# The product of stick weight and running product on GpSimd in the attention stage

## The chip, the cores and the metric

The kernel runs on one core of a Trainium2 chip. The core's engines are TensorE (PE in the profile, its weight loads PEld), VectorE (DVE), ScalarE (ACT), GpSimd (POOL) and SyncE (SP, which issues the DMAs here). The metric is the time of one execution on the device in microseconds; lower is better. Times of one kernel are given as the median of its runs.

## The reference

One layer of a streaming encoder with 2048 tokens of 1024 channels: a normed input, one large projection, an SSD scan branch and an attention branch of 16 heads with 64 channels each, gates, an output projection and a residual. The change concerns the attention alone, which is "stick breaking": a key's weight is its own sigmoid times the product of the failure probabilities of all keys between it and the query.

```python
def stick_breaking(q, k, v):
    ...
    for blk in range(L // SB_BLOCK):
        ...
        logits = jnp.einsum('bqhd,bkhd->bhqk', q[:, q0:kend], k[:, :kend]).astype(jnp.float32) * scale
        ...
        mask = ki < qi
        log_fail = jnp.where(mask, jax.nn.log_sigmoid(-logits), 0.0)
        between = lax.cumsum(log_fail, axis=3, reverse=True) - log_fail
        w = jnp.where(mask, jnp.exp(jax.nn.log_sigmoid(logits) + between), 0.0)
        outs.append(jnp.einsum('bhqk,bkhd->bqhd', w.astype(v.dtype), v[:, :kend]))
```

## The kernel before

The kernel keeps float32 precision on TensorE by splitting operands into a high part and a rest, so most products are three matmuls and most evictions come with a subtraction (a "split") on VectorE. Its stages follow one another: norm and first projections, values, the SSD branch, the attention stage (about 930 to 2660 us), and the output stage.

The attention stage works through 160 steps. A step is (head, 512 queries `qs`, 512 keys `kc`), the keys from the last block to the first; ten steps make a head. Four of them are diagonal (`kc == qs`): their units are 128, 256, 384 and 512 keys wide. The other six are full. Each step has four units, one for each 128 queries. `attn_qk` (L829) makes a unit:

- TensorE writes the logits `lg` (L839, L840). ScalarE makes from them the failure probabilities, sigmoid(-x), into `tc` (L843), a tile one column wider than the unit, whose last column a GpSimd memset (L842) has set to 1; and the stick weights, sigmoid(x), into `sw` (L845).
- On the diagonal GpSimd masks the last 128 columns of both (L847, L849).
- VectorE runs a scan over `tc` from right to left (L852), which turns it into running products. Its start value is the carry of the step before, `cy`.
- The product `sw * tc`, shifted by one column (L853), is the attention weight. It is written over `sw`. This is the line that changes.
- If more keys follow, GpSimd copies the first column of `tc` into `cy` (L856); the unit with the same queries of the next step reads it.

`attn_tr` (L862) turns 128 keys of all four units of a step on TensorE (L868), which needs the products of all four units; ScalarE copies the result to `wh` (L870) and VectorE subtracts the rest into `wl` (L872, one input in PSUM). `attn_av` (L875) multiplies with the values. Between these, `fill` gives TensorE matmuls of projections that are not needed yet (`proj`), with weight splits on VectorE (L134) and evictions.

What sets the order: TensorE's instructions are chained in the order in which the code issues them. In step s this is, for i = 0 to 3, the transposes of 128 keys of step s, the logits of unit i of step s+1, the value products two behind, and fill. So the logits of step s+1 stand behind transposes that wait for the last product of step s. On the other engines the scheduler puts the instructions in a fixed order at build time, and each engine takes them strictly one after another. There are five `tc` tiles and six `sw` tiles; a memset for a unit can run as soon as the product and the copy five units earlier are done with the tile.

At the start of the last head's query blocks the first part of the output stage's norm work is mixed in (`first_y`, L739): squares on ScalarE, additions (L695) and splits (L684) on GpSimd.

Of the kernel before, what the change touches and what calls it, by code (L numbers as in the profile page):

```python
# [14 lines left out]
ALU = mybir.AluOpType  # L15
# [33 lines left out]
def hybrid_kernel(ctx, tc, x, norm_pre, w_in, b_gate, conv_w, conv_b, dt_bias, a_log, d_skip,  # L49
                  ssd_norm, w_ssd_proj, w_sb_proj, w_out, norm_post, out, dbg=None):  # L50
    nc = tc.nc
# [21 lines left out]
    def matmul(*a, **k):  # L73
        chain(nc.tensor.matmul(*a, **k))  # L74
# [754 lines left out]
    def attn_qk(s, i):  # L829
        if s >= len(steps):  # L830
            return
        h, qs, kc = steps[s]
        diag = kc == qs
        W = (i + 1) * P if diag else TB
        qa, qb = qts[h, qs]
        k = kts[h, kc]
        qc = slice(i * P, (i + 1) * P)
        lg = ap.tile([P, TB], F32, name="lg", tag="lg", bufs=2)
        matmul(lg[:, :W], qa[:, qc], k[:, :W], start=True, stop=False)  # L839
        matmul(lg[:, :W], qb[:, qc], k[:, :W], start=False, stop=True)  # L840
        t = ab.tile([P, TB + 1], F32, name="tc", tag="tc", bufs=5)
        nc.gpsimd.memset(t[:, W:W + 1], 1.0)  # L842
        nc.scalar.activation(t[:, :W], lg[:, :W], AF.Sigmoid, scale=-0.125)  # L843
        w = ab.tile([P, TB], F32, name="sw", tag="sw", bufs=6)
        nc.scalar.activation(w[:, :W], lg[:, :W], AF.Sigmoid, scale=0.125)  # L845
        if diag:
            nc.gpsimd.affine_select(out=t[:, W - P:W], in_=t[:, W - P:W], compare_op=ALU.is_gt, fill=1.0, base=0,  # L847
                                    pattern=[[-1, P]], channel_multiplier=1)
            nc.gpsimd.affine_select(out=w[:, W - P:W], in_=w[:, W - P:W], compare_op=ALU.is_gt, fill=0.0, base=0,  # L849
                                    pattern=[[-1, P]], channel_multiplier=1)  # L850
        tr = t[:, W::-1]
        nc.vector.tensor_tensor_scan(tr, tr, tr, 1.0 if diag else carry[h, qs, i], ALU.mult, ALU.min)  # L852
        nc.vector.tensor_mul(w[:, :W], w[:, :W], t[:, 1:W + 1])  # L853
        if kc > 0:
            c = ab.tile([P, 1], F32, name="cy", tag="cy", bufs=8)
            nc.gpsimd.tensor_copy(c, t[:, 0:1])  # L856
            carry[h, qs, i] = c
        ws[s, i] = w
# [39 lines left out]
    for tb in range(NTB):  # L898
        if tb == NTB - 1:
            for i in range(CPB):  # L900
                later(1 + 6 * i, lambda i=i: attn_qk(0, i))
        run(proj(wg, tb, done_g(0, tb)))
    flush()
    for s in range(len(steps)):
        attn_load(s + 2)
        for i in range(CPB):
            attn_tr(s, i)
            attn_qk(s + 1, i)
            if i >= 2:
                attn_av(s, i - 2)  # L910
            fill(i)
        for i in range(2, CPB):
            attn_av(s, i)
            fill(i + 2)
# [153 lines left out]
```

## Time and profile before

| | |
|---|---|
| median of 3 runs | 3164.92 us (3163.69 to 3165.49) |
| span of the profiled execution, first to last instruction | 3163.6 us |
| PE busy | 3024.1 us, 96% |
| DVE busy | 2457.2 us, 78% |
| ACT busy | 1585.7 us, 50% |
| POOL busy | 477.9 us, 15% |

The profiled execution's own time is not listed apart from its span; the median of the runs is 1.3 us above that span. Busy shares are averages over stages of different make. The chain of work that ended last is followed back from the last instruction, at each step to what released it. In a timeline a row gives start, duration, engine, line, operation, output and inputs; where the engine was idle before, the idle time and what ended it stand in brackets. Recorded ends of matmuls are modelled.

### The profile page before, as it was taken

The numbers are of one execution on the slowest core, as the hardware profiler recorded it, in microseconds if no ns is written. First come the engines' busy times: TensorE is split into PE (matmuls) and PEld (weight loads), VectorE is DVE, ScalarE is ACT, GpSimd is POOL, SyncE is SP. The second block draws the span as 40 slices with busy tenths as digits, with TensorE's granted clock in tenths as the row PEclk, the third lists the DMA queues.
The fourth block names the chain that finished last, engine by engine and source line by source line (L and its number), as shares of the span: only waits on it lengthen the run. The fifth ranks groups of instructions, "written<-read, shape, count | busy, mean of one in ns | idle before, by whom it ended". The sixth has DMA issues, their size and how long they took to land.

```text
span 3163.6 us, 48155 instructions
## 1 busy us (share of the span) xinstructions
PE 3024.1 (96%) x16169; PEld 2496.9 (79%) x16169; DVE 2457.2 (78%) x4357; ACT 1585.7 (50%) x3102; POOL 477.9 (15%) x1626
## 2 busy tenths in 40 slices
PE   8999999999999999999999999999999989999998
PEld 6899888787877777777777777777777767888887
DVE  7321688768869989989899999989998899756553
ACT  6211345434446666566565666566665656333321
POOL 0000011100111212122212121222111231101000
PEclk9999999999999999999999999999999999999999
DMA  5532022212243334224323333334233334555452
GB/s 165 148 122 93 24 71 80 68 40 67 72 128 89 90 89 110 80 81 113 93 70 103 94 97 91 87 94 114 69 89 90 111 117 144 176 148 167 133 167 70
DMA packets 298816, 320.63 MB, mean 101 GB/s; under 512 B 23148, under 2 KB 187848, under 8 KB 298568
## 3 DMA queue, kind: packets, MB, share of 16 engines
q1 hardware_dynamic: 298416, 317.51, 34.6%
q8 instruction: 128, 2.10, 0.3%
q14 instruction: 120, 0.98, 0.1%
q10 hardware_dynamic: 152, 0.05, 0.0%
HBM read 216.67 MB, written 100.79 MB: 100 GB/s over the span
## 4 chain that ended last, share of the span: by engine, by line
PE 53%; DVE 33%; issue 5%; DMA 4%; ACT 4%; POOL 1%; SPq 0%; DVEq 0%; POOLq 0%; ACTq 0%
PE proj L74 30%; DVE tc L852 13%; PE po L74 8%; DVE sw L853 7%; PE vps L74 6%; DVE wl L872 5%; PE wtp L77 4%; PE lg L74 3%; DMA csb<-csd 2%; ACT sw L845 1%; ACT wh L870 1%; PE yp L74 1%; DVE acc L474 1%; DVE o L893 1%; DVE o L892 1%
## 5 line engine op out<-in xcount | busy, mean ns | idle before, releaser
L74 PE MATMUL proj<-hh,whi 128*128 128x512 f32 x1920 | 762.0, 397 | 0.1
L74 PE MATMUL proj<-hh,wlo 128*128 128x512 f32 x1920 | 761.7, 397 | 0.0
L74 PE MATMUL proj<-hl,whi 128*128 128x512 f32 x1920 | 760.4, 396 | 1.3 <-DVE hl L286 1.1
L870 ACT CAST wh<-wtp 128x512 fp32r<-128x512 f32 (+3 forms) x640 | 337.1, 527 | 390.2 <-PE wtp L77 386.6
L852 DVE TENSOR_TENSOR_SCAN tc<-tc,cy 128x513 f32<-128x513 f32 x384 | 490.9, 1278 | 0.3 <-ACT tc L843 0.3
L872 DVE TENSOR_TENSOR wl<-wtp,wh 128x512 fp32r<-128x512 f32 (+3 forms) x640 | 383.0, 599 | 81.5 <-ACT wh L870 80.3
L77 PE MATMUL wtp<-ident,sw 128*128 128x128 f32 x2176 | 369.9, 277 | 72.2 <-DVE sw L853 70.1
L853 DVE TENSOR_TENSOR sw<-sw,tc 128x512 f32<-128x512 f32 (+3 forms) x640 | 394.2, 616 | 50.5 <-POOL sw L849 13.5
L77 PEld LDWEIGHTS wtp<-ident,sw 128*128 128x128 f32 x2176 | 280.7, 141 | 181.0 <-DVE sw L853 99.1
L74 PEld LDWEIGHTS proj<-hl,whi 128*128 128x128 f32 x1920 | 362.6, 189 | 72.6 <-DVE hl L286 2.5
L74 PEld LDWEIGHTS proj<-hh,wlo 128*128 128x128 f32 x1920 | 362.6, 189 | 70.7 <-issue 0.3
L74 PEld LDWEIGHTS proj<-hh,whi 128*128 128x128 f32 x1920 | 362.7, 189 | 70.1 <-ACT hh L285 0.5
L845 ACT ACTIVATE sw<-lg 128x512 f32<-128x512 f32 (+3 forms) x640 | 346.1, 541 | 49.8 <-PE wtp L77 49.6
L843 ACT ACTIVATE tc<-lg 128x512 f32<-128x512 f32 (+3 forms) x640 | 349.1, 545 | 18.7 <-PE lg L74 13.1
L132 ACT CAST whi<-wraw 128x512 fp32r<-128x512 f32 x248 | 154.3, 624 | 280.5 <-PE proj L74 178.9
L74 PE MATMUL lg<-kt,qa 128*128 128x512 f32 (+3 forms) x640 | 285.1, 445 | 0.0
L74 PE MATMUL po<-wl,vt 128*128 128x512 f32 (+3 forms) x640 | 242.6, 379 | 29.0 <-DVE wl L872 28.2
L852 DVE TENSOR_TENSOR_SCAN tc<-tc 128x129 f32<-128x129 f32 (+3 forms) x256 | 218.1, 852 | 26.3 <-POOL tc L847 25.2
L74 PE MATMUL lg<-kt,qb 128*128 128x512 f32 (+3 forms) x640 | 234.6, 367 | 0.0
L74 PE MATMUL po<-wh,vt 128*128 128x512 f32 (+3 forms) x640 | 232.4, 363 | 0.0
L134 DVE TENSOR_TENSOR wlo<-wraw,whi 128x512 fp32r<-128x512 f32 x246 | 173.4, 706 | 73.3 <-ACT whi L132 70.5
L856 POOL COPY cy<-tc 128x1 f32<-128x1 f32 x384 | 133.6, 348 | 448.7 <-DVE tc L852 448.7
(202 smaller groups left out, 4887.8 us busy)
## 6 DMA issues: line engine op xcount, KB each, us to landing
wraw<-in_w_in SPq DMA_DIRECT2D x120, 256.0 KB, 3.0
vst<-vt SPq DMA_DIRECT2D x64, 256.0 KB, 2.0
csb<-csd SPq DMA_DIRECT2D x64, 256.0 KB, 4.4
qa<-qst SPq DMA_DIRECT2D x64, 256.0 KB, 3.5
qb<-qst SPq DMA_DIRECT2D x128, 128.0 KB, 3.8
kt<-kst SPq DMA_DIRECT2D x64, 256.0 KB, 3.2
vt<-vst SPq DMA_DIRECT2D x64, 256.0 KB, 3.0
gtd<-zb SPq DMA_DIRECT2D x64, 256.0 KB, 2.1
```

The source lines that it names most:

```text
L74: chain(nc.tensor.matmul(*a, **k))
L77: chain(nc.tensor.transpose(*a))
L132: nc.scalar.copy(h, raw)
L134: (eng or nc.vector).tensor_tensor(l, raw, h.bitcast(F32), op=ALU.subtract)
L474: nc.vector.scalar_tensor_tensor(acc, xp[:, i:i + TB], pv[:, col:col + 1], acc, op0=ALU.mult, op1=ALU.add)
L843: nc.scalar.activation(t[:, :W], lg[:, :W], AF.Sigmoid, scale=-0.125)
L845: nc.scalar.activation(w[:, :W], lg[:, :W], AF.Sigmoid, scale=0.125)
L852: nc.vector.tensor_tensor_scan(tr, tr, tr, 1.0 if diag else carry[h, qs, i], ALU.mult, ALU.min)
L853: nc.vector.tensor_mul(w[:, :W], w[:, :W], t[:, 1:W + 1])
L856: nc.gpsimd.tensor_copy(c, t[:, 0:1])
L870: nc.scalar.copy(wh[:, lo:], tp[:, lo:])
L872: nc.vector.tensor_sub(wl[:, lo:], tp[:, lo:], wh[:, lo:].bitcast(F32))
```

## The change

The product of line 853 is issued on GpSimd instead of VectorE, with the same operands and shapes, 640 times (448 of them 512 wide). Nothing else in the source differs.

```diff
         nc.vector.tensor_tensor_scan(tr, tr, tr, 1.0 if diag else carry[h, qs, i], ALU.mult, ALU.min)
-        nc.vector.tensor_mul(w[:, :W], w[:, :W], t[:, 1:W + 1])
+        nc.gpsimd.tensor_tensor(w[:, :W], w[:, :W], t[:, 1:W + 1], op=ALU.mult)
         if kc > 0:
```

TensorE's order is the same. VectorE's order in a full step, before (head 5, query block 3, key block 1; numbers at names count tiles):

```order
L852 SCALAR_TENSOR_TENSOR tc_15373<-tc_15373,cy_15260 128x513
L853 TENSOR_TENSOR sw_15376<-sw_15376,tc_15373 128x512
L872 TENSOR_TENSOR wl_15392<-wtp_15385,wh_15390 128x512
L852 SCALAR_TENSOR_TENSOR tc_15397<-tc_15397,cy_15283 128x513
L872 TENSOR_TENSOR wl_15416<-wtp_15409,wh_15414 128x512
L853 TENSOR_TENSOR sw_15400<-sw_15400,tc_15397 128x512
L852 SCALAR_TENSOR_TENSOR tc_15421<-tc_15421,cy_15305 128x513
```

And the same place of VectorE's order after the change:

```order
L852 SCALAR_TENSOR_TENSOR tc_15373<-tc_15373,cy_15260 128x513
L872 TENSOR_TENSOR wl_15392<-wtp_15385,wh_15390 128x512
L852 SCALAR_TENSOR_TENSOR tc_15397<-tc_15397,cy_15283 128x513
L872 TENSOR_TENSOR wl_15416<-wtp_15409,wh_15414 128x512
L852 SCALAR_TENSOR_TENSOR tc_15421<-tc_15421,cy_15305 128x513
```

The products are gone from VectorE; one split stands between two scans.

VectorE's order after the change around a weight split, one step later (query block 3, key block 0):

```order
L852 SCALAR_TENSOR_TENSOR tc_15543<-tc_15543,cy_15428 128x513
L134 TENSOR_TENSOR wlo_16197<-wraw_16193,whi_16195 128x512
L872 TENSOR_TENSOR wl_15562<-wtp_15555,wh_15560 128x512
L852 SCALAR_TENSOR_TENSOR tc_15567<-tc_15567,cy_15454 128x513
L134 TENSOR_TENSOR wlo_16203<-wraw_16199,whi_16201 128x512
```

The weight split L134 stands directly behind a scan.

GpSimd's order in a diagonal step before (head 5, query and key block 2):

```order
L847 AFFINE_SELECT tc_15623<-tc_15623 128x128
L849 AFFINE_SELECT sw_15626<-sw_15626 128x128
L856 COPY cy_15634<-tc_15623 128x1
L842 MEMSET tc_15788 128x1
L847 AFFINE_SELECT tc_15651<-tc_15651 128x128
L849 AFFINE_SELECT sw_15654<-sw_15654 128x128
L856 COPY cy_15662<-tc_15651 128x1
```

And after the change:

```order
L847 AFFINE_SELECT tc_15623<-tc_15623 128x128
L849 AFFINE_SELECT sw_15626<-sw_15626 128x128
L853 TENSOR_TENSOR sw_15626<-sw_15626,tc_15623 128x128
L856 COPY cy_15634<-tc_15623 128x1
L842 MEMSET tc_15788 128x1
L847 AFFINE_SELECT tc_15651<-tc_15651 128x128
L849 AFFINE_SELECT sw_15654<-sw_15654 128x128
L853 TENSOR_TENSOR sw_15654<-sw_15654,tc_15651 128x256
L856 COPY cy_15662<-tc_15651 128x1
```

The product of a unit stands between the mask of its own `sw` and the carry copy; the masks of the next unit stand behind both.

## Rows read from the trace of the kernel before

**Rows 1.** The page: busy times and instructions, the chain by line, the product's group.

```profile
PE 3024.1 (96%) x16169; PEld 2496.9 (79%) x16169; DVE 2457.2 (78%) x4357; ACT 1585.7 (50%) x3102; POOL 477.9 (15%) x1626
...
PE proj L74 30%; DVE tc L852 13%; PE po L74 8%; DVE sw L853 7%; PE vps L74 6%; DVE wl L872 5%; PE wtp L77 4%; PE lg L74 3%; DMA csb<-csd 2%; ACT sw L845 1%; ACT wh L870 1%; PE yp L74 1%; DVE acc L474 1%; DVE o L893 1%; DVE o L892 1%
...
L853 DVE TENSOR_TENSOR sw<-sw,tc 128x512 f32<-128x512 f32 (+3 forms) x640 | 394.2, 616 | 50.5 <-POOL sw L849 13.5
```

**Rows 2.** The attention stage as one window: stretch, busy us (instructions), clock, DMA.

```profile
938.00:2658.00 1720.00, 1615.87 (x8189) 1298.88 (x8189) 1569.01 (x2239) 1055.87 (x2217) 378.75 (x1533) 0.99 0.33 94
```

**Rows 3.** VectorE's groups by form in that window: count, busy us, mean ns.

```profile
L852 DVE TENSOR_TENSOR_SCAN tc<-tc 128x385 f32<-128x385 f32 x63 | 61.0, 968 | 2.9 <-POOL tc L847 2.8
L134 DVE TENSOR_TENSOR wlo<-wraw,whi 128x512 fp32r<-128x512 f32 x84 | 58.7, 699 | 0.0
L852 DVE TENSOR_TENSOR_SCAN tc<-tc 128x257 f32<-128x257 f32 x63 | 47.7, 758 | 1.1
...
L852 DVE TENSOR_TENSOR_SCAN tc<-tc 128x129 f32<-128x129 f32 x63 | 26.6, 422 | 0.4 <-POOL tc L847 0.4
```

**Rows 4.** The timeline of a full step, from its first scan to the next step's.

```profile
1482.16 1.28 DVE L852 TENSOR_TENSOR_SCAN tc<-tc,cy 128x513 f32<-128x513 f32 x1
...
1483.51 0.19 POOL L856 COPY cy<-tc 128x1 f32<-128x1 f32 x1 [2.77 <-DVE tc L852]
...
1491.11 0.69 DVE L853 TENSOR_TENSOR sw<-sw,tc 128x512 f32<-128x512 f32 x1
...
1491.86 0.33 PE L77 MATMUL wtp<-ident,sw 128*128 128x128 f32 x1 [0.23 <-DVE sw L853]
...
1491.94 0.48 PE L74 MATMUL lg<-kt,qa 128*128 128x512 f32 x1
...
1492.75 0.60 ACT L843 ACTIVATE tc<-lg 128x512 f32<-128x512 f32 x1
1492.84 0.69 DVE L872 TENSOR_TENSOR wl<-wtp,wh 128x512 fp32r<-128x512 f32 x1 [0.44 <-ACT wh L870]
...
1493.45 1.28 DVE L852 TENSOR_TENSOR_SCAN tc<-tc,cy 128x513 f32<-128x513 f32 x1
```

**Rows 5.** All scans of line 852 on the diagonal: first and last start.

```profile
L852 DVE TENSOR_TENSOR_SCAN tc<-tc x256: 409/864/1342, 930.4 to 2655.7; 128x129 f32<-128x129 f32 x64, 128x385 f32<-128x385 f32 x64
```

**Rows 6.** The timeline of a diagonal step: memset and mask on GpSimd between two scans.

```profile
1572.17 0.10 POOL L842 MEMSET tc<- 128x1 f32 x1 [0.27 <-DVE sw L853]
1572.28 0.29 POOL L847 TENSOR_SCALAR_AFFINE_SELECT tc<-tc 128x128 f32<-128x128 f32 x1
```

**Rows 7.** Timelines of three places where GpSimd and VectorE work beside each other.

```profile
1541.62 0.94 DVE L852 TENSOR_TENSOR_SCAN tc<-tc 128x385 f32<-128x385 f32 x1
1541.66 1.00 POOL L849 TENSOR_SCALAR_AFFINE_SELECT sw<-sw 128x128 f32<-128x128 f32 x1 [0.34 <-ACT sw L845]
...
2558.43 1.27 DVE L852 TENSOR_TENSOR_SCAN tc<-tc,cy 128x513 f32<-128x513 f32 x1
2558.51 2.27 POOL L684 TENSOR_TENSOR yl<-mp,yh 128x512 fp32r<-128x512 f32 x1
2559.62 0.26 DVE L872 TENSOR_TENSOR wl<-wtp,wh 128x128 fp32r<-128x128 f32 x1
...
2513.91 1.72 POOL L695 TENSOR_TENSOR scr<-scr 128x512 f32<-128x512 f32 x1
...
2514.62 2.09 DVE L852 TENSOR_TENSOR_SCAN tc<-tc,cy 128x513 f32<-128x513 f32 x1
```

**Rows 8.** GpSimd's full-width two-input operations: one alone, then lines with min/median/max ns.

```profile
2518.43 1.27 POOL L695 TENSOR_TENSOR mp<-mp 128x512 f32<-128x512 f32 x1
...
L976 POOL TENSOR_TENSOR scr<-scr x16: 1262/1293/1300, 2725.7 to 3158.4; 128x512 f32<-128x512 f32 x16
...
L695 POOL TENSOR_TENSOR scr<-scr x21: 1284/1294/1727, 2506.1 to 2982.3; 128x512 f32<-128x512 f32 x21
...
L506 POOL TENSOR_TENSOR xe<-xd,dec x32: 1062/1376/3569, 385.1 to 897.8; 128x512 f32<-128x512 f32 x32
```

## The prediction

> **What bounds the kernel now.** I read the page's busy shares first, then one window over the attention stage, then one step of that stage instruction by instruction, then the places where GpSimd and VectorE meet.
>
> The page has TensorE busy for 96% of the span and VectorE for 78% [rows 1]. Neither average decides. In the chain that ended last, the line of the scan (L852) has 13% and the product that is to move (L853) 7%, GpSimd 1% [rows 1]. All of L853 lies in the attention stage, 938 to 2658 us; there TensorE is recorded busy for 1615.87 of 1720 us, VectorE for 1569.01 and GpSimd for 378.75 [rows 2]. So VectorE looks full and GpSimd looks free, and an average would credit the change with the 394.2 us of the 640 products [rows 1].
>
> One step shows what the time is made of [rows 4]. A step is four units; a unit is a scan and then its product. The scan of unit 0 starts at 1482.16 and the product of unit 3 ends at 1491.11 + 0.69 = 1491.80. These 9.64 us are a chain on VectorE: scan, product and a split (L872), one behind another. Then TensorE, which runs in a fixed order, transposes that last product (1491.86), and only behind this can it make the next step's logits (1491.94). ScalarE makes the failure probability from them at 1492.75, and the next scan starts at 1493.45. I call the 1.65 us from 1491.80 to 1493.45 the **restart**: it is paid once a step and holds nothing that the change touches (the VectorE split at 1492.84 lies beside ScalarE's work). A step is 9.64 + 1.65 = 11.29 us. From first scan to last, 160 steps take 2655.7 - 930.4 = 1725.3 us [rows 5]; counted as 159.5 steps that is 10.82 us a step, 108.2 us a head of ten steps (six full ones, four diagonal ones whose widths are 128, 256, 384 and 512).
>
> So the question is not how busy VectorE is, but how long four scans and four products take when a product is on the other engine.
>
> **What two engines do when both read SBUF.** The rows answer. At 1541.66 a mask on GpSimd that takes 0.29 us elsewhere [rows 6] takes 1.00: it began just behind a scan that ran from 1541.62 to 1542.56 and ended 0.10 after it [rows 7]. At 2558.51 a GpSimd subtraction (full width, two inputs) took 2.27 us: the scan beside it ended at 2559.70, the subtraction at 2560.78, that is 1.08 later [rows 7]. In the other direction the scan of 2514.62, on which nothing in its own inputs had to wait, took 2.09 us and ended at 2516.71, 1.08 us after the GpSimd addition that ended at 2515.63 [rows 7]. Each waits until the other has ended; they share no time except some 0.2 us of start-up. A split whose input comes from PSUM (L872) isn't held in this way: at 2559.62 it took its usual 0.26 while that subtraction was under way [rows 7]. Hence a scan and a full-width product on GpSimd take turns.
>
> **The price of the product on GpSimd.** A full-width two-input operation of GpSimd takes 1.27 us alone in this stage; the medians are 1.293 and 1.294 over 16 and 21 additions and 1.376 over 32 products of an earlier stage, with 1.26 the least of the additions [rows 8]. I take 1.28, because the additions have two dense inputs and are written over one of them, as here. Bounds: 1.26 and 1.38. (The 1.06 that one of the 32 products took is no bound: an input of them is a broadcast.) For narrow products no row exists; between a one-element copy (0.18 to 0.19) [rows 4] and 1.28 for 512 a straight line gives 0.46, 0.73 and 1.00 us for 128, 256 and 384.
> The Trainium skill (GPSIMD Engine Reference, section 3.1) measures a two-input elementwise operation on GpSimd at 1.96 times VectorE's time. By that ratio the product would cost an estimated 1.96 x 0.69 = 1.35 us, and the sum below would come out some 38 us higher; the row of 1.27 in this very stage decides against it.
>
> **A full step after the change.** Unit 0: scan 1.28, hand-over 0.06 (the copy at 1483.51 starts 0.07 behind its scan [rows 4]), product 1.28: 2.62 us. In VectorE's order a split stands between two scans, so the product gets its turn first, and the next scan ends 1.08 behind it, then 0.06, then 1.28: 2.42 us, three times. Together 2.62 + 7.26 = 9.88 us, with the splits (0.69 [rows 4]) hidden beside the products. With the restart 11.53 us, where this step had 11.29. The carry copy is queued behind the product on GpSimd; as in the row at 1541.66 it ends about with the next scan, and its reader comes four units later: nothing. The memsets of 0.10 us [rows 6] are for a unit five further on and delay nobody.
> The weight splits L134 (84 in the stage, two inputs in SBUF [rows 3]) take their turn too. They stand directly behind a scan in VectorE's order and so go ahead of the product, at 0.60 us each (0.70 recorded, some 0.1 of it beside the instruction ahead): 50 us over 160 steps, 0.31 a step. A full step is then 11.84 us.
>
> **A diagonal step.** Here GpSimd's own order makes a loop: product n, carry copy, memset, mask of tc n+1, and only behind that scan n+1. Scans 0.42 + 0.76 + 0.97 + 1.26 = 3.41 [rows 3]; products 0.46 + 0.73 + 1.00 + 1.28 = 3.47; hand-overs 4 x 0.06 = 0.24; three times copy 0.14, memset 0.11, mask 0.29 and hand-over 0.04 [rows 6], 1.74. Sum 8.86, and 8.76 in the mean, since 16 of the 64 diagonal steps have no copy. With restart and weight splits 10.72 us. What is queued on GpSimd behind the waiting product is thus what VectorE waits for next.
>
> **Sum.** A head: 6 x 11.84 + 4 x 10.72 = 113.9 us against 108.2, and 16 x 5.7 = 91 us. In the last head GpSimd also has six additions and eight subtractions of the output stage's first part (L695, L684); each is a further turn of up to 1.27 us in its queue, 0 to 18 us, of which I take 10, since they delay the products of today too. The removed VectorE time (394 us) gives nothing back elsewhere: what it did was in this chain, and its place is taken. TensorE does the same work and only waits longer; the waiting moves from VectorE's product to GpSimd's. The profiled execution's span is 3163.6 us and the median of the runs 3164.9, 1.3 apart. 3163.6 + 101 + 1.3 = 3266: **3266 us**, 3.2% slower.
>
> **Rivals.**
> A, **the turns are not needed** for this pair, or the product hides. Then the chain of a full step is four scans with four splits and one last product, 4 x (1.28 + 0.68) + 0.06 + 1.28 = 9.18, with the restart 10.83; a diagonal one is 8.76 + 1.65 = 10.41. A head is 106.6 us, 26 us less over 16; where scans start before their predecessors' records end it is shorter still, but TensorE's recorded 1615.87 us, 10.1 a step, hold the gain to 16 x (108.2 - 101) = 115. In the middle 3095 us, faster. It decides if a product and a scan can run side by side. For it speaks VectorE's 91% in the stage; against it every row of [rows 7]. Chance 0.08. The Trainium skill (Perfetto Trace Analysis, section Optimizing Scalar/DVE Operations) says that with VectorE saturated, moving work even to GpSimd may make sense, and warns that the two share an SBUF read port; the first half is this rival, and the rows go with the warning.
> B, **the product is dearer**: it reads tc from its second word (1 to W), which no GpSimd operation of this trace does. At 1.60 us a full step pays 4 x 0.32 and a diagonal one, by width, 2.5 x 0.32 more: 96 x 1.28 + 64 x 0.80 = 174 us, 3440. Chance 0.08.
> C, **a part is hidden**: weight splits beside the products (-50) and the diagonal loop no dearer than today's mean step (-30), the last head at nothing (-10) and the cheapest product (-11) leave 3165, no change. Chance 0.04.
> The forecast has 0.80.
>
> **Range and chances.** Within the forecast, 1.26 instead of 1.28 gives -11, weight splits half hidden -25, the last head at nothing -10, narrow products below the straight line (0.29 us for 128, as the one-input mask) -25; 1.38 gives 0.40 a full step and 0.25 a diagonal one, +54, the last head at 18 +8, the 33 masks of sw that stand behind a carry copy in the new order at 0.43 each +14, and up to 35 for turns that fall badly. So 3195 to 3377. That leaves out A, C and most of B, 2 in 10. Faster by over 0.2% (about what a measurement of this kernel can tell) 0.08, within it 0.04, slower 0.88.
>
> **What would show it.** L853 on GpSimd near 1.3 us in the median; recorded scans of 513 well above 1.28 us in the mean, about 1.8, because they are issued behind a split while the product still holds; GpSimd near 1100 us busy in the stage and above 15% of the chain; a full step of 11.5 to 12 us; the restart still 1.65. Scans that stay at 1.28 beside running products would prove the turns wrong; a median product above 1.4 would prove B.

## The result and the profile after

The changed kernel takes **3257.63 us** (median of 4 runs, 3254.18 to 3268.18) where the kernel before takes 3165.03 (4 runs, 3163.69 to 3165.49): the ratio is 1.030, with an interval of 1.0283 to 1.0316. It is 92.6 us slower; 101 had been forecast, with a range of 30 to 212.

The page of the changed kernel: busy times, then the group of the product and the group of the scans of full steps (the same columns as in [rows 1]).

```profile
PE 3049.6 (94%) x16169; PEld 2518.5 (77%) x16169; DVE 2265.9 (70%) x3717; ACT 1588.0 (49%) x3102; POOL 1159.9 (36%) x2266
...
L853 POOL TENSOR_TENSOR sw<-sw,tc 128x512 f32<-128x512 f32 (+3 forms) x640 | 664.3, 1038 | 598.3 <-DVE tc L852 351.5
...
L852 DVE TENSOR_TENSOR_SCAN tc<-tc,cy 128x513 f32<-128x513 f32 x384 | 620.6, 1616 | 5.1 <-ACT tc L843 3.6
```

VectorE gave away 394 us of products [rows 1], and its busy time fell by only 2457.2 - 2265.9 = 191 us. Much of the rest is in the second row: the 384 scans of full steps now have 1616 ns in the mean, where one took 1.28 us in [rows 4]: 384 x 0.34 = 129 us. They do no more work; they wait inside the record.

The attention stage of the changed kernel as one window (columns as in [rows 2]), and from the same stretch the products by width and the weight split.

```profile
944.00:2750.00 1806.00, 1637.25 (x8189) 1317.80 (x8189) 1381.02 (x1602) 1058.22 (x2217) 1057.44 (x2171) 0.98 0.32 89
...
L853 POOL TENSOR_TENSOR sw<-sw,tc 128x512 f32<-128x512 f32 x448 | 538.3, 1202 | 505.8 <-DVE tc L852 262.8 <-PE proj L74 96.3 <-ACT wh L870 48.7
...
L853 POOL TENSOR_TENSOR sw<-sw,tc 128x384 f32<-128x384 f32 x63 | 55.4, 879 | 21.0 <-DVE tc L852 17.3
L853 POOL TENSOR_TENSOR sw<-sw,tc 128x256 f32<-128x256 f32 x63 | 41.1, 653 | 42.4 <-DVE tc L852 42.3
L853 POOL TENSOR_TENSOR sw<-sw,tc 128x128 f32<-128x128 f32 x63 | 27.3, 433 | 27.0 <-DVE tc L852 27.0
...
L134 DVE TENSOR_TENSOR wlo<-wraw,whi 128x512 fp32r<-128x512 f32 x84 | 78.2, 932 | 5.2 <-ACT whi L132 3.2 <-PE proj L74 1.0 <-PE wtp L77 0.5
```

The stage has grown from 1720 to 1806 us. TensorE, the fullest, has 1637 of 1806 us (91%, before 94%), VectorE 76% (91%); GpSimd has more than before, but only 59% (22%). That is the picture of a chain over two engines, not of one engine at its limit.

The timeline of the step that stands in [rows 4], after the change (start, duration, engine, line; in brackets the idle time before it and what ended it).

```profile
1517.47 1.28 DVE L852 TENSOR_TENSOR_SCAN tc<-tc,cy 128x513 f32<-128x513 f32 x1
...
1518.93 1.09 POOL L853 TENSOR_TENSOR sw<-sw,tc 128x512 f32<-128x512 f32 x1 [2.82 <-DVE tc L852]
...
1519.25 1.85 DVE L852 TENSOR_TENSOR_SCAN tc<-tc,cy 128x513 f32<-128x513 f32 x1
...
1519.96 1.12 POOL L856 COPY cy<-tc 128x1 f32<-128x1 f32 x1
1521.27 1.10 POOL L853 TENSOR_TENSOR sw<-sw,tc 128x512 f32<-128x512 f32 x1
...
1526.02 1.09 POOL L853 TENSOR_TENSOR sw<-sw,tc 128x512 f32<-128x512 f32 x1 [1.09 <-DVE tc L852]
...
1528.76 1.29 DVE L852 TENSOR_TENSOR_SCAN tc<-tc,cy 128x513 f32<-128x513 f32 x1
```

Here is what had been forecast, move by move. The scan ends at 1518.75 and the product starts at 1518.93. It ends at 1520.02. The next scan, recorded from 1519.25, doesn't take its 1.28 us from there: it ends at 1521.10, 1.08 behind the product. The copy issued at 1519.96 takes 1.12 us where it took 0.19 [rows 4], and ends at 1521.08, with the scan. The last product ends at 1527.11 and the next step starts at 1528.76: a restart of 1.65, the number of before.

And yet this step takes 1528.76 - 1517.47 = 11.29 us, exactly what it took in [rows 4]. So it isn't here that the 92 us are. For that I took every step of the stage from the timelines, from its first scan to the first scan of the next, and sorted them: 48 full steps behind a full step, 48 full steps behind a diagonal one, 64 diagonal ones (the last of them has no step behind it and is left out of the means). The chain is from the first scan to the end of the last product; the rest is the restart. Means in us:

| steps | before: step (chain + restart) | after: step (chain + restart) | difference, times count |
|---|---|---|---|
| full behind full | 11.61 (9.93 + 1.68) | 11.51 (9.83 + 1.68) | -0.10 x 48 = -5 |
| full behind diagonal | 10.61 (8.86 + 1.75) | 11.73 (9.94 + 1.79) | +1.12 x 48 = +54 |
| diagonal | 10.32 (7.89 + 2.43) | 10.95 (9.14 + 1.80) | +0.63 x 64 = +40 |

Together 89 of the 92.6 us. Why the first two rows differ is seen in the second unit of a step behind a diagonal one. First the kernel before, with the splits beside that unit, then the changed one.

```profile
1473.31 0.52 DVE L872 TENSOR_TENSOR wl<-wtp,wh 128x384 fp32r<-128x384 f32 x1
...
1474.36 1.27 DVE L852 TENSOR_TENSOR_SCAN tc<-tc,cy 128x513 f32<-128x513 f32 x1
...
1475.55 0.39 DVE L872 TENSOR_TENSOR wl<-wtp,wh 128x256 fp32r<-128x256 f32 x1
1475.87 0.68 DVE L853 TENSOR_TENSOR sw<-sw,tc 128x512 f32<-128x512 f32 x1
1476.47 1.27 DVE L852 TENSOR_TENSOR_SCAN tc<-tc,cy 128x513 f32<-128x513 f32 x1
...
1477.67 0.26 DVE L872 TENSOR_TENSOR wl<-wtp,wh 128x128 fp32r<-128x128 f32 x1
```

```profile
1508.59 1.28 DVE L852 TENSOR_TENSOR_SCAN tc<-tc,cy 128x513 f32<-128x513 f32 x1 [0.47 <-ACT tc L843]
...
1509.79 0.40 DVE L872 TENSOR_TENSOR wl<-wtp,wh 128x256 fp32r<-128x256 f32 x1
...
1510.05 1.09 POOL L853 TENSOR_TENSOR sw<-sw,tc 128x512 f32<-128x512 f32 x1 [1.23 <-DVE tc L852]
...
1510.36 1.86 DVE L852 TENSOR_TENSOR_SCAN tc<-tc,cy 128x513 f32<-128x513 f32 x1 [0.17 <-ACT tc L843]
```

The splits (L872) in a step belong to the weights of the step before. Behind a full step they are 512 wide, 0.69 us each on VectorE's chain; behind a diagonal one they are 512, 384, 256 and 128 wide, and the three narrow ones cost 0.52, 0.39 and 0.26. Against three of 0.69 that is 0.90 of the 1.07 us by which the chain of before is shorter there. After the change the splits lie beside the product and are free, at any width, and both kinds of full step have the same chain, 9.83 and 9.94. A wide split that becomes free pays for the turn; a narrow one doesn't.

The diagonal step shows the loop through GpSimd's queue.

```profile
1495.99 0.41 POOL L853 TENSOR_TENSOR sw<-sw,tc 128x128 f32<-128x128 f32 x1 [0.68 <-DVE tc L852]
...
1496.35 0.18 POOL L856 COPY cy<-tc 128x1 f32<-128x1 f32 x1
...
1496.59 0.10 POOL L842 MEMSET tc<- 128x1 f32 x1
1496.69 0.29 POOL L847 TENSOR_SCALAR_AFFINE_SELECT tc<-tc 128x128 f32<-128x128 f32 x1
1496.93 0.29 POOL L849 TENSOR_SCALAR_AFFINE_SELECT sw<-sw 128x128 f32<-128x128 f32 x1
1497.02 0.76 DVE L852 TENSOR_TENSOR_SCAN tc<-tc 128x257 f32<-128x257 f32 x1 [0.72 <-POOL tc L847]
```

Product, copy, memset, mask, and only then the next scan: 0.62 us from the product's end at 1496.40 to the scan at 1497.02 (0.58 forecast), and VectorE idle for 0.72. Over the stage, from the waits of the kernel before and then of the changed one (total us, times, longest):

```profile
PE wtp L77 <- DVE sw L853: 69.8, 91, 2.3
DVE tc L852 <- POOL tc L847: 7.9, 26, 0.8
...
PE wtp L77 <- POOL sw L853: 145.5, 170, 3.2
DVE tc L852 <- POOL tc L847: 125.4, 154, 1.6
```

VectorE waits 125 us for that mask, where it had waited 7.9. TensorE's wait for the product has moved from VectorE's line to GpSimd's and grown from 70 to 146 us.

### The profile page after: what moved, and what is told of

Its sections match the earlier page's. It is cut to its first block, busy times and chain, and to the rows that moved or that the text cites. A ratio compares the mean times of both kernels' runs of the same rounds, so it can differ in the third digit from the quotient of the medians.

```text
span 3258.2 us, 48215 instructions
## 1 busy us (share of the span) xinstructions
PE 3049.6 (94%) x16169; PEld 2518.5 (77%) x16169; DVE 2265.9 (70%) x3717; ACT 1588.0 (49%) x3102; POOL 1159.9 (36%) x2266
## 5 line engine op out<-in xcount | busy, mean ns | idle before, releaser
L853 POOL TENSOR_TENSOR sw<-sw,tc 128x512 f32<-128x512 f32 (+3 forms) x640 | 664.3, 1038 | 598.3 <-DVE tc L852 351.5
L852 DVE TENSOR_TENSOR_SCAN tc<-tc,cy 128x513 f32<-128x513 f32 x384 | 620.6, 1616 | 5.1 <-ACT tc L843 3.6
L872 DVE TENSOR_TENSOR wl<-wtp,wh 128x512 fp32r<-128x512 f32 (+3 forms) x640 | 380.6, 595 | 272.2 <-ACT wh L870 269.5
L77 PE MATMUL wtp<-ident,sw 128*128 128x128 f32 x2176 | 389.4, 281 | 151.1 <-POOL sw L853 147.6
L506 POOL TENSOR_TENSOR xe<-xd,dec 128x512 f32<-128x512 f32 x32 | 50.4, 1574 | 837.1 <-DVE xd L504 837.1
L134 DVE TENSOR_TENSOR wlo<-wraw,whi 128x512 fp32r<-128x512 f32 x246 | 191.6, 780 | 80.1 <-ACT whi L132 71.4
```

What stands on the lines that cost most here:

```text
L77: chain(nc.tensor.transpose(*a))
L134: (eng or nc.vector).tensor_tensor(l, raw, h.bitcast(F32), op=ALU.subtract)
L506: nc.gpsimd.tensor_tensor(heads(xe), heads(xd), tok(dec), op=ALU.mult)
L853: nc.gpsimd.tensor_tensor(w[:, :W], w[:, :W], t[:, 1:W + 1], op=ALU.mult)
L872: nc.vector.tensor_sub(wl[:, lo:], tp[:, lo:], wh[:, lo:].bitcast(F32))
```

## The experiments

**Is it the turns, or GpSimd's slower product?** The scan's second operand only caps the running product at itself, and the products don't exceed 1; so a 1.0 serves as well. Put into PSUM, it leaves the scan with one operand in SBUF. GpSimd has the same 2266 instructions as in the changed kernel, in the same order but for a few. `e_cap_pool` has the product on GpSimd, `e_cap_dve`, its control, on VectorE. The cap takes a PSUM bank, so the weights' transposes (`wtp`) have two banks instead of three in both.

```
+    cap = ap.tile([P, 8], F32, name="cap", bufs=1)
+    nc.vector.tensor_copy(cap, ones[:, 0:8])
...
-        nc.vector.tensor_tensor_scan(tr, tr, tr, 1.0 if diag else carry[h, qs, i], ALU.mult, ALU.min)
-        nc.vector.tensor_mul(w[:, :W], w[:, :W], t[:, 1:W + 1])
+        nc.vector.tensor_tensor_scan(tr, tr, cap[:, 0:1].to_broadcast([P, W + 1]), 1.0 if diag else carry[h, qs, i],
+                                    ALU.mult, ALU.min)
+        nc.gpsimd.tensor_tensor(w[:, :W], w[:, :W], t[:, 1:W + 1], op=ALU.mult)     # e_cap_dve: nc.vector
...
-        tp = ap.tile([P, TB], F32, name="wtp", tag="wtp", bufs=3)
+        tp = ap.tile([P, TB], F32, name="wtp", tag="wtp", bufs=2)
```

> The product is on GpSimd as in the changed kernel, but the scan's second input (the cap of 1.0) is one PSUM element broadcast, so the scan reads only one input from SBUF; one transpose bank in PSUM is given up for it (wtp 2 instead of 3). Turns theory: scan and product run side by side, recorded scans of 513 stay near 1.3 us, a full step falls from 11.6 to about 10.4 us, diagonal steps stay near 10.9, the time falls to 3120 to 3180 us. Rival (only the longer way over GpSimd costs, hand-over and product, no turns): 3240 to 3280 us, full steps stay at 11.6.

Measured: 3103.69 us (3100.68 to 3105.34), 0.9803 of before (0.9788 to 0.9817). First rows from the timeline of a full step, then the line of the 384 full scans (their inputs are `tc`, the carry and `cap`; min/median/max ns):

```profile
1463.84 1.28 DVE L854 TENSOR_TENSOR_SCAN tc<-tc,cy,cap 128x513 f32<-128x513 f32 x1
...
1465.29 1.09 POOL L856 TENSOR_TENSOR sw<-sw,tc 128x512 f32<-128x512 f32 x1 [3.13 <-DVE tc L854]
...
1465.79 1.28 DVE L854 TENSOR_TENSOR_SCAN tc<-tc,cy,cap 128x513 f32<-128x513 f32 x1
...
1467.25 1.09 POOL L856 TENSOR_TENSOR sw<-sw,tc 128x512 f32<-128x512 f32 x1 [0.58 <-DVE tc L854]
```

```profile
L854 DVE TENSOR_TENSOR_SCAN tc<-tc,cy,cap x384: 1259/1274/1283, 940.7 to 2574.3; 128x513 f32<-128x513 f32 x192
```

The product from 1465.29 to 1466.38 and the scan from 1465.79 to 1467.07 lie beside each other, and both take their time alone, 1.09 and 1.28. Of 384 scans none takes more than 1.283 us. The turns are gone with the scan's second SBUF operand, and with them the loss.

> Control for e_cap_pool: the product on VectorE as before, with the scan's cap in PSUM and two transpose banks. Both theories: the scan keeps its 1.28 us, nothing takes turns with GpSimd but masks and copies; 3155 to 3200 us, the surplus over 3165 being the price of the lost PSUM bank.

Measured: 3146.58 us (3144.57 to 3147.71), ratio 0.9939 (0.9924 to 0.9954). The forecast missed: the control is not equal to before, it is 20 us faster. The masks and copies of GpSimd also read SBUF, and they no longer meet a scan; the copies show it, 348 ns in the mean before and 294 here.

```profile
L856 POOL COPY cy<-tc 128x1 f32<-128x1 f32 x384 | 133.6, 348 | 448.7 <-DVE tc L852 448.7
...
L859 POOL COPY cy<-tc 128x1 f32<-128x1 f32 x384 | 113.0, 294 | 449.0 <-DVE tc L854 449.0
```

How the 20 us divide over masks, copies and scans wasn't separated. Against this control the move of the product is worth 3146.6 - 3103.7 = 43 us of gain; with the scan as it was, the same move costs 92.6. So turns at the scan are worth 135 us to it.

**Is a bank less of `wtp` part of that?** `e_wtp2` is the kernel before with `bufs=2` in that one line.

> The kernel before with two transpose banks in PSUM instead of three and nothing else, the second half of the control: it splits the 20 us that the cap run with the product on VectorE gained. If the gain is the cap's (masks and copies no longer meet the scan), this is 3160 to 3190 us; if it comes with the two banks, 3140 to 3150 us.

Measured: 3165.05 us over 10 runs (3161.51 to 3169.88), ratio 1.0003 (0.9993 to 1.0012). No change beyond the noise. So the 20 us come with the cap, not with the bank.

**Which steps pay.** The product moves in one kind of step only.

```
+        (nc.gpsimd if diag else nc.vector).tensor_tensor(w[:, :W], w[:, :W], t[:, 1:W + 1], op=ALU.mult)  # e_diag_only
+        (nc.vector if diag else nc.gpsimd).tensor_tensor(w[:, :W], w[:, :W], t[:, 1:W + 1], op=ALU.mult)  # e_full_only
```

> The product on GpSimd in the diagonal steps only. Here a scan stands behind GpSimd's mask, the mask behind the copy and the product of the unit before: +0.63 us on 64 steps, 3165 + 40 = about 3205 us (3190 to 3220). Rival (turns are the whole cost): in a diagonal step scan and product never meet, so 3165 to 3180 us.

Measured: 3204.86 us (3203.31 to 3210.23), ratio 1.0132 (1.0117 to 1.0147), 41 us above before. By steps: full ones 11.60 and 10.65, as before; diagonal ones 10.93, that is 0.61 x 64 = 39 us. The waits of the scans for the mask (us, times), in the kernel before and in this one:

```profile
  POOL tc L847: 25.2, 30
...
  POOL tc L847: 145.9, 158
```

The scan waits for the mask behind the product, and there the loss is: the loop through GpSimd's queue stands.

> The product on GpSimd in the six full steps of a head, on VectorE in the four diagonal ones. Turns theory with the step times of the two traces: full steps behind a diagonal one +1.1 us (48 of them), the other full steps unchanged, diagonal steps as before: 3165 + 54 = about 3215 us (3195 to 3230). Rival (the queue of GpSimd, which holds the masks behind the product, is the whole cost): full steps have no masks, so 3165 to 3180 us.

Measured: 3241.53 us (3236.86 to 3243.47), ratio 1.0243 (1.0228 to 1.0258), 77 us above before and more than forecast. By steps: 11.61 for a full one behind a full one, as before; 12.00 behind a diagonal one, 1.39 x 48 = 67 us; 10.43 for a diagonal one, 0.11 x 64 = 7. That is the same split into two kinds as in the table above. It is even dearer than in the changed kernel (12.00 against 11.73), and the timeline of a step behind a diagonal one shows one reason:

```profile
1495.08 1.27 DVE L852 TENSOR_TENSOR_SCAN tc<-tc,cy 128x513 f32<-128x513 f32 x1
1496.27 0.52 DVE L872 TENSOR_TENSOR wl<-wtp,wh 128x384 fp32r<-128x384 f32 x1
1496.53 5.25 POOL L853 TENSOR_TENSOR sw<-sw,tc 128x512 f32<-128x512 f32 x1 [3.66 <-ACT wh L870]
1496.72 1.27 DVE L852 TENSOR_TENSOR_SCAN tc<-tc,cy 128x513 f32<-128x513 f32 x1
...
1498.23 1.26 DVE L852 TENSOR_TENSOR_SCAN tc<-tc,cy 128x513 f32<-128x513 f32 x1
...
1499.61 1.27 DVE L852 TENSOR_TENSOR_SCAN tc<-tc,cy 128x513 f32<-128x513 f32 x1
```

The product is recorded from 1496.53, before the scan of 1496.72, and still it waits through three scans and ends at 1501.78, 0.90 behind the third. All three other products of the step then come after the last scan. In the changed kernel no product took longer than 2.10 us. What lets the scans pass isn't how far ahead the product is recorded: here it is 0.19 us, and the changed kernel has 73 products with a scan recorded 0.01 to 0.22 us behind them, each of which went first. In `e_full_only` 8 of 72 such products were passed, all of them the first of their step, at 0.195 to 0.21 us, where other first products with the same distance went ahead. What decides it stays open. Ten of the 48 steps behind a diagonal one have a product of over 2.2 us; the other 38 take 11.72 us in the mean, as in the changed kernel (11.73). So these ten steps are 0.28 x 48 = 13 of the 26 us by which the run lies above its forecast, and the diagonal steps are 7.

The two parts alone add to 41 + 77 = 118 us, and the whole change costs 92.6: they are not independent.

**The turns measured by a dead operation.** The kernel before stays as it is, and behind each product GpSimd gets extra work on a tile that nobody else uses: in `e_dead_mul` a product of the same width, in `e_dead_set` two memsets, which only write.

```
+    dead = ab.tile([P, TB], F32, name="dead", bufs=1)
+    nc.gpsimd.memset(dead, 1.0)
...
         nc.vector.tensor_mul(w[:, :W], w[:, :W], t[:, 1:W + 1])
+        nc.gpsimd.tensor_tensor(dead[:, :W], dead[:, :W], dead[:, :W], op=ALU.mult)   # e_dead_mul
+        nc.gpsimd.memset(dead[:, :W], 1.0)                                            # e_dead_set, twice
```

> The kernel before, and behind each product on VectorE one GpSimd product of the same width over a tile that nobody else reads or writes; nothing waits for its result. Turns theory: each one holds VectorE's scan or product back by up to 1.1 us, some of it in gaps: 3250 to 3500 us, scans recorded well over 1.28 us. Rival (only the way over GpSimd costs): no one waits for it, 3160 to 3190 us.

> Control for e_dead_mul: two GpSimd memsets of the same tile and width in the place of the dead product, about 0.5 us each, which read nothing. Both theories: 3160 to 3190 us, since GpSimd has the time and the scan doesn't meet a reader; if GpSimd's queue alone were the cost, this would be as slow as e_dead_mul.

Measured: 3614.85 us (3612.76 to 3617.51, ratio 1.1418) and 3254.98 us (3252.83 to 3257.85, ratio 1.0282). Both are above what either theory gave, so as a measure of the turns this pair failed; why, the groups say. First `e_dead_set`: the full scans from 931 to 1654 us, the diagonal scans of the whole run, the line of one of the two memsets, and the stretch as one window (columns as in [rows 2]). Then `e_dead_mul`: the full scans from 950 to 1691 us, the dead product's line, and the window.

```profile
L854 DVE TENSOR_TENSOR_SCAN tc<-tc,cy 128x513 f32<-128x513 f32 x144 | 183.9, 1277 | 0.4 <-ACT tc L845 0.4
...
L854 DVE TENSOR_TENSOR_SCAN tc<-tc 128x129 f32<-128x129 f32 (+3 forms) x256 | 217.3, 849 | 113.3 <-POOL tc L849 108.7 <-POOL tc L844 3.1
...
L856 POOL MEMSET dead<- x640: 198/524/534, 914.2 to 1652.6; 128x512 f32 x96, 128x128 f32 x64
...
931.00:1654.00 723.00, 625.19 (x3037) 484.77 (x3036) 577.61 (x817) 387.64 (x815) 672.86 (x1818) 0.98 0.30 80
```

```profile
L854 DVE TENSOR_TENSOR_SCAN tc<-tc,cy 128x513 f32<-128x513 f32 x72 | 131.9, 1832 | 44.5 <-POOL cy L859 43.2 <-ACT tc L845 0.8 <-ACT sw L847 0.3
...
L856 POOL TENSOR_TENSOR dead<-dead x640: 392/1039/2882, 917.6 to 1691.0; 128x512 f32<-128x512 f32 x96, 128x128 f32<-128x128 f32 x64
...
950.00:1691.00 741.00, 395.76 (x1476) 294.70 (x1476) 411.30 (x396) 192.67 (x395) 707.71 (x881) 0.71 0.14 39
```

The extra work doesn't stand where it was meant to. The scheduler put all memsets into the first six heads, where GpSimd is busy 673 of 723 us, and the masks stand behind them in GpSimd's order: the scan waits 108.7 us for the mask, 25.2 before. So the 88 us of this run are a price of the queue without any turn, but of a queue far denser than that of the changed kernel. The 640 dead products all lie in the first three heads. There GpSimd is busy 708 of 741 us, TensorE's granted clock is 0.71, and a head takes 238 to 259 us where it takes 105 to 107 before; the later heads take what they took before. So the 448 us of this run come from a stretch in which GpSimd has nearly no idle time left, and no price of the turns can be read from them, nor from the 360 us between the two runs. What the pair does show is in the scan's own records: 1832 ns in the mean beside the products, which read, and 1277 beside the memsets, which only write.

**The version that keeps the gains.** The cap in PSUM takes the turns away; the loop of the diagonal step remains (10.72 us in `e_cap_pool` against 10.17 in `e_cap_dve`). So the product goes to GpSimd in full steps only, with the cap: `e_cap_full`, which differs from `e_cap_pool` in

```
+        (nc.vector if diag else nc.gpsimd).tensor_tensor(w[:, :W], w[:, :W], t[:, 1:W + 1], op=ALU.mult)
```

> A version meant to be faster than both kernels: the scan's cap in PSUM (no turns) and the product on GpSimd in full steps only (no loop through the masks). From the step times of the cap runs: full steps as with cap and GpSimd, diagonal steps 10.17 instead of 10.72 us, 64 of them: 3104 - 35 = about 3070 us (3055 to 3090). If TensorE is late in those steps anyway, 3095 to 3110 us.

Measured: 3059.61 us (3058.32 to 3062.09), ratio 0.9671 (0.9657 to 0.9686): as forecast, 105 us faster than before and 198 faster than the changed kernel. Its attention stage as one window:

```profile
930.00:2560.00 1630.00, 1595.28 (x8268) 1311.63 (x8267) 1333.12 (x1873) 1063.82 (x2235) 726.58 (x1932) 1.00 0.36 101
```

TensorE is now recorded busy for 98% of the stage, so little seems left to win on the other engines. All kernels by steps, in us, from the timelines as in the table above:

| kernel | full behind full | full behind diagonal | diagonal | median |
|---|---|---|---|---|
| before | 11.61 | 10.61 | 10.32 | 3165.0 |
| changed | 11.51 | 11.73 | 10.95 | 3257.6 |
| `e_cap_dve` | 11.49 | 10.49 | 10.17 | 3146.6 |
| `e_cap_pool` | 10.60 | 9.74 | 10.72 | 3103.7 |
| `e_cap_full` | 10.61 | 9.57 | 10.17 | 3059.6 |
| `e_full_only` | 11.61 | 12.00 | 10.43 | 3241.5 |
| `e_diag_only` | 11.60 | 10.65 | 10.93 | 3204.9 |
| `e_dead_set` | 12.37 | 10.85 | 10.96 | 3255.0 |
| `e_dead_mul` | 16.37 | 12.33 | 12.22 | 3614.9 |

The rows of the two dead runs mix the heads that hold the extra work with those that don't.

## Why the prediction was right

It was right in direction and nearly in size (+101 forecast, +92.6 measured), and its mechanism is shown. That the size is so near is in part luck, since several terms were off in opposite directions. Point by point, in its order:

- **The turns of scan and product** (from [rows 7]): shown. They stand in the timeline of the changed kernel, and `e_cap_pool`, which removes what makes them and nothing of GpSimd's work, turns +92.6 into -63. Rival A, that the turns are not needed, is what that run is; it needed a change to the scan.
- **The next scan ends 1.08 behind the product**: 1520.02 to 1521.10, exact. **The restart stays 1.65**: 1527.11 to 1528.76, exact; 1.68 and 1.79 in the mean of full steps.
- **The product at 1.28 us**: too dear. Alone it takes 1.09; the 1202 ns of the group hold waits. The bounds of 1.26 and 1.38 didn't contain it, and the one row below them in [rows 8], 1.06, had been set aside because it has a broadcast operand. Rival B, a dearer product, is refuted with it. **The hand-over at 0.06**: too cheap, 0.17 to 0.18 from the scan's end to the product (1518.75 to 1518.93, 1521.10 to 1521.27). Product and hand-over together are 1.26 or 1.27 instead of 1.34, so the two errors nearly cancel. The Trainium skill (GPSIMD Engine Reference, section 3.1) has 1.96 for GpSimd's time over VectorE's, measured on an addition of 2048 elements; for the 512-wide product here it is 1.09 / 0.69 = 1.58.
- **Full step 11.84**: 11.62 measured, the mean of 11.51 and 11.73; the chain is 9.88 in the mean, where the sum had 9.88 + 0.31 for the weight splits. They do take their turns (L134 has 932 ns, before 699 [rows 3]), but what of that reaches the chain wasn't separated from the cheaper product. What the prediction didn't see is that the cost falls on one half of the full steps: it worked out one full step for all and compared heads (108.2), and its sample step of [rows 4] is of the half that loses nothing.
- **Diagonal step 10.72**: 10.95 measured. The chain is 9.14 (9.07 forecast), the restart 1.80 instead of 1.65. The loop through GpSimd is shown by `e_diag_only`. The narrow products took 0.43, 0.65 and 0.88 us, somewhat under the straight line's 0.46, 0.73 and 1.00. Of the 1.25 us by which the chain grew, 0.62 came out of the restart, which had been 2.43.
- **The sum.** Steps: 91 us forecast, 89 measured (a head 113.5 us, 113.9 forecast; before 107.9). By kind it was less near: against the measured steps of before, the forecast had (11.84 - 11.11) x 96 = 70 us for the full steps and (10.72 - 10.32) x 64 = 26 for the diagonal ones; measured are 49 and 40. The 10 us for the last head didn't come: it grew by 5.2 us, the other fifteen by 5.5 in the mean. The profiled executions differ by 94.6 us: 86.7 from first scan to last, 5.2 before the first scan and 2.7 behind the last; why the scans begin 5.2 us later wasn't looked into.
- **A reading.** The prediction has all of L853 after 938 us; the first product starts at 931.0. No term hangs on it.
- **The signs.** Full scans 1616 ns in the mean (about 1800 forecast); GpSimd 1057 us busy in the stage (about 1100); L853 with a median of 1.09 (1.3). GpSimd's share of the chain that ended last could not be read: the page follows that chain back only over the last part of the span, and its shares sum to 17% (TensorE 15%, VectorE and GpSimd 1% each).
- **In part open: TensorE's clock.** The prediction had no term for it. Over the whole run of the changed kernel the granted clock has a mean of 0.986 of 2.4 GHz; the kernel before had 0.993. As time that is 3258.2 x 0.014 = 46 us lost against 3163.6 x 0.007 = 22, so some 24 us more. The steps bound how much of it can lie on the chain. Those in which the clock stayed at its upper level throughout (150 of the 159 before, 127 after) have 11.59, 10.43 and 10.13 us before (in the order of the table) and 11.39, 11.41 and 10.77 after: times the counts that is 79 of the 89 us. So some 10 us lie in the steps in which the clock fell to 1.2 GHz; whether the clock made them long or their waits made it fall can't be told from these runs. TensorE idled more in the changed kernel (its 91% of the stage), and in `e_cap_full`, where it idles least, the stage has 1.00.

## What to carry to other kernels

Before giving VectorE's work to GpSimd, look at what VectorE does meanwhile: if that reads two operands from SBUF, as the scan here, and the moved work reads SBUF too, expect the two to take turns, with the slower engine's time put into the chain, less what becomes free beside it; find the rows where they already meet. Price each kind of step by itself: here one kind lost nothing, and a sample step of it hid the cost. If one operand can be put into PSUM (here a constant that the operation only needs as a cap), the same move changes its sign, from +92.6 to -43 us. And look at what is queued behind the moved work on GpSimd: where its next masks feed the next step, leave the work where it is.

## What the runs showed of the hardware beyond that

- A scan whose second operand is a broadcast word in PSUM costs no more than one with both in SBUF: median 1.274 us for 513 columns against 1.28, and it runs beside GpSimd's product at full speed on both sides. The Trainium skill (SBUF — State Buffer, section Who interferes with whom) says that a VectorE instruction with two SBUF inputs contends with a GpSimd one that reads SBUF, and not with one that only writes it, and that one with at most one SBUF input, outside the two-port modes, doesn't contend. The scans of 1.85 us beside products in the changed kernel, those of 1277 ns beside the memsets of `e_dead_set` and those of 1274 ns beside products in `e_cap_pool` agree.
- Who gets the turn isn't who is recorded first: the product of 5.25 us was recorded 0.19 us before the first of the three scans that went ahead of it, while all 73 products of the changed kernel with a scan recorded 0.01 to 0.22 us behind them went first.
- A 512-wide product of GpSimd that reads one operand from its second word takes 1.09 us, less than the 1.27 to 1.29 of its 512-wide additions [rows 8]. The second word isn't what makes it cheap: the 448 dead products of this width in `e_dead_mul`, of a tile with itself from its first word, have a median of 1.04. Whether it is the operation was not tried.
